# A hybrid decoder block on one core: mLSTM by chunks with a state, four GLA levels in blocks of 32, a rebuilt end, and sums of MLP weights made by adding transfers

## The chip, the core and the metric

The kernel runs on one NeuronCore of a Trainium2 chip. Five engines work at once on a shared on-chip memory of 128 partitions: TensorE (PE in the rows; its weight loads are PEld), VectorE (DVE), ScalarE (ACT), GpSimd (POOL) and SyncE (SP, which here only issues transfers). Each engine takes its own instructions strictly in order, and waits on semaphores for the others. PSUM is the memory that TensorE writes its products to. The metric is the device time of one execution in microseconds (us).

## What is computed

One layer (DEPTH = 1) of a decoder with 512 tokens of width 1024. Three token mixers work side by side on the normed input (mLSTM, GLA and gated DeltaNet, each with 4 heads of 128), are merged by sigmoid gates, and are followed by a squared-ReLU MLP of width 4096 and a last norm.

```
u = rmsnorm(x, g_norm_mix);  proj = u @ w_in            # q, k, v, gates of all three mixers
# mLSTM, per head, over chunks, with carried C, n, m
P   = exp(D - m_t) * (q k^T)                             # D from cumulated forget gates and input gates
num = P v + w_inter * (q C);  den = sum(P) + w_inter * (q n)
h   = num / max(|den|, exp(-m_t))
C   = w_old * C + (k * w_s)^T v                          # the state that the next chunk gets
# GLA, per head, decay per channel, b = cumsum(g) in a chunk
A[t,s] = sum_k q[t,k] exp(b[t,k] - b[s,k]) k[s,k]        # s <= t
o   = A v + (q exp(b)) S;   S = exp(bL) S + (k exp(bL - b))^T v
# gated DeltaNet: a triangular solve per chunk, then a state as above
x = x + (sum_n sigmoid(gate_n) * (branch_n @ w_up_n)) @ w_out
u = rmsnorm(x, g_norm_mlp)
x = x + square(relu(u @ w_mlp_in)) @ w_mlp_out
return rmsnorm(x, g_final)
```

## The kernel before

**Who sets the order.** The program is recorded as a graph of operations (`Graph.record`, L160), each with a cost per engine (`cost`, L207). `schedule` (L247) plays the graph through with these costs, and the order in which operations start there is the order in which each engine gets them (`emit`, L511). So nothing is ordered at run time: an instruction whose input is late holds up all that stands behind it on its engine. Large matmul groups ("mains") come in a fixed sequence of names (`plan`, L544 to L550); the small matmuls of the mixers are put between them when their inputs should be there. Buffers come in classes with a fixed count: the halves of a split weight (`wh`, `wl`) have 3 each, the mixers' PSUM banks (`m`) have 4.

**Products in fp32 by three.** Large products split each operand into a rounded half and a rest, and make three matmuls of 512 columns (`mm3`, L611). A weight that arrives by DMA is cast by ScalarE (`...h`) and its rest is made by VectorE (`...l`), as in `split_b`, L1438. Small products of the mixers are plain fp32 matmuls, which the trace shows as two instructions each.

**mLSTM** (`gen_mlstm`, L1133). No state is carried. For each head the 512 x 512 lower triangle of weighted scores is made in four block columns (`mqk`, with 512, 384, 256 and 128 columns), and ten products with the values (`mn`, 129 columns, the last of them for the denominator) follow.

**GLA** (`gen_gla`, L1205). Inside a chunk of 128 the lower triangle of A is made by levels of halves: at level L the queries of the second half and the keys of the first half of every stretch of 2L tokens are scaled to the border between them. Levels 64, 32 and 16 make small products, one for each stretch. Levels 8, 4, 2 and 1 make one product of 128 x 64 for each of four chunks (`ll`), of which a mask picks what counts (`copy_predicated` into `lAT`).

**MLP.** `mlp_in` (L1417) makes 512 hidden columns in four quarters (`mip`, 24 matmuls each). `mlp_out` (L1445) multiplies each such group with its part of the second weight by a scheme of Strassen and Winograd's kind, seven half-size products (`product`, 12 matmuls each, named P1 to P7; tiles `P` and `pp`) in place of eight. The four quarters of the weight, `b11` to `b22`, are transferred into the tile `em` by SP, and the four sums of quarters that the scheme needs are made by VectorE in place, as `em<-em`. Seven groups go this way, the eighth is `mlp_last` (L1529).

**End.** For each of four blocks of 128 tokens (t), two halves of 512 columns (hf): the last product is added to `x2`, ScalarE takes the squares' sum (`square_of`), and `finish` (L1563) makes the norm's factor `fy` from a square root on ScalarE and one Newton step on VectorE, multiplies by factor and weight (`gf`), and stores.

Of the kernel before, what the change touches and what calls it, by code (L numbers as in the profile page):

```python
# [113 lines left out]
class Graph:  # L114
# [92 lines left out]
    def cost(self, eng, method, a, k, op):  # L207
# [364 lines left out]
def write_block(nc, xT, w_cm, w_tm, w_sc, w_up, w_out, w_mi, w_mo, w_lr, prm, cst, g_fin, x_tm, out):  # L572
# [560 lines left out]
    def gen_mlstm(h):  # L1133
# [4 lines left out]
        pt = []  # L1138
        for j in range(4):
            e = nc.tile("w", [P, S], F32, f"me{h}{j}")  # L1140
            bias = a_c[:, h, j:j + 1]
            nc.scalar.activation(e[:, blk(j)], md[:, blk(j)], AF.Exp, bias=bias)
            if j < 3:
                nc.scalar.activation(e[:, (j + 1) * P:], nm[:, (j + 1) * P:], AF.Exp, bias=bias)
            pq = mps(f"mqk{h}{j}")
            mm(pq[:, j * P:], mk[h][:, blk(j)], mq[h][:, j * P:])
            nc.vector.tensor_mul(e[:, j * P:], e[:, j * P:], pq[:, j * P:])
            pt.append(e)
# [46 lines left out]
    hlT = []  # L1195
    cone = slot("cone")
# [8 lines left out]
    def gen_gla(h):  # L1205
        if h == 0:
            lrr = tmp("lrr")
            nc.sync.dma_start(lrr[:96], w_lr)
            nc.scalar.copy(lrw[:96], lrr[:96])
            nc.gpsimd.memset(cone, 1.0)  # L1210
            nc.gpsimd.memset(h4(cone)[:, :, 0:1], 0.0)
            nc.vector.tensor_sub(lrw[64:96], lrr[64:96], lrw[64:96].bitcast(F32))
# [32 lines left out]
        for li_, L in enumerate((64, 32, 16, 8, 4, 2, 1)):  # L1245
            nb = S // (2 * L)
            b3 = b.rearrange("p (n x) -> p n x", x=2 * L)
            w = nc.tile("w", [P, S], F32, f"lw{h}{L}")
            w3 = w.rearrange("p (n x) -> p n x", x=2 * L)
            k3 = lk[h].rearrange("p (n x) -> p n x", x=2 * L)  # L1250
            q3 = lq[h].rearrange("p (n x) -> p n x", x=2 * L)
            nc.vector.tensor_sub(w3[:, :, :L + 1], b3[:, :, L:L + 1].broadcast_to([P, nb, L + 1]), b3[:, :, :L + 1])
            if L > 1:
                nc.vector.tensor_sub(w3[:, :, L + 1:], b3[:, :, L + 1:], b3[:, :, L:L + 1].broadcast_to([P, nb, L - 1]))
            nc.scalar.activation(w, w, AF.Exp, scale=-1.0 / 16.0)
            q_ = q3[:, :, L:]
            if L > 1:
                wq = nc.tile("mq", [P, 256], F32, f"lwq{h}{L}").rearrange("p (n l) -> p n l", l=L)
                nc.vector.tensor_mul(wq, w3[:, :, L:], q_)
                q_ = wq  # L1260
            nc.vector.tensor_mul(w3[:, :, :L + 1], w3[:, :, :L + 1], k3[:, :, :L + 1])
            pl = mps(f"ll{h}{L}")
            p4 = pl[:, :256].rearrange("p (c n l) -> p c n l", c=4, l=L)
            nh = 64 // L
            if L >= 16:
                for c in range(4):
                    for i in range(nh):
                        o = c * P + i * 2 * L
                        mm(p4[i * 2 * L:i * 2 * L + L + 1, c, i], w[:, o:o + L + 1], q_[:, c * nh + i])
# [4 lines left out]
                for i in range(nh):  # L1274
                    r0 = i * 2 * L
                    nc.either.copy(A4[r0:r0 + L + 1, :, r0 + L:r0 + 2 * L], p4[r0:r0 + L + 1, :, i])
            else:
                for c in range(4):
                    mm(p4[:, c], w[:, blk(c)], q_[:, c * nh:(c + 1) * nh])
                nc.vector.copy_predicated(At.rearrange("p (c n x) -> p c n x", c=4, x=2 * L)[:, :, :, L:], lmask(li_ - 3), p4)  # L1280
# [92 lines left out]
    r2n = one("r2n", [P, 2])  # L1373
    r2c = one("r2c", [P, 4])

    def gen_x2():
# [14 lines left out]
        nc.vector.tensor_scalar_mul(r2n, r2c[:, 2:4], -1.0)  # L1391
# [53 lines left out]
    def mlp_out(g, a):  # L1445


        (a11, a21), (a12, a22) = a
        b11, b12, b21, b22 = bq
        for x, hf, i in ((b11, 0, 0), (b12, 1, 0), (b22, 1, 1), (b21, 0, 1)):  # L1450
            nc.sync.dma_start(x, w_mo[g, hf, i])

        tail = g == NG - 2
# [17 lines left out]
        product(1, a11, b11, "11")  # L1471
        if tail:
            for t in range(2):
                us[t] = slot(f"u{t}")
                nc.either.copy(us[t], p1[t])
        s1 = slot("S1")
        nc.vector.tensor_add(s1, a21, a22)
        nc.vector.tensor_sub(b11, b12, b11)
        for t, ps in enumerate(product(5, s1, b11, "S1")):
            if g == 0:  # L1480
                p5[t] = slot(f"P5{t}")
                nc.either.copy(p5[t], ps)
            else:
                nc.vector.tensor_add(p5[t], p5[t], ps)
        s2 = slot("S2")
        nc.vector.tensor_sub(s2, s1, a11)
        nc.vector.tensor_sub(a21, a11, a21)
        nc.vector.tensor_sub(b12, b22, b12)
        for t, ps in enumerate(product(7, a21, b12, "S3")):
            if g == 0:  # L1490
                p7[t] = slot(f"P7{t}")
                nc.either.copy(p7[t], ps)
            else:
                nc.vector.tensor_add(p7[t], p7[t], ps)
        nc.vector.tensor_sub(b11, b22, b11)
        product(6, s2, b11, "S2")
        if tail:
            join()
        s4 = slot("S4")
        nc.vector.tensor_sub(s4, a12, s2)  # L1500
        for t, ps in enumerate(product(3, s4, b22, "S4")):
            if tail:
                break
            nc.vector.scalar_tensor_tensor(x2[t][1], ps, r2c[:, t:t + 1], x2[t][1], op0=ALU.mult, op1=ALU.add)
        nc.vector.tensor_sub(b11, b11, b21)
        for t, ps in enumerate(product(4, a22, b11, "22")):
            nc.vector.scalar_tensor_tensor(x2[2 + t][0], ps, r2n[:, t:t + 1], x2[2 + t][0], op0=ALU.mult, op1=ALU.add)
        for t, ps in enumerate(product(2, a12, b21, "12")):
            if tail:
                break  # L1510
            nc.vector.scalar_tensor_tensor(x2[t][0], ps, r2c[:, t:t + 1], x2[t][0], op0=ALU.mult, op1=ALU.add)

    def join():

        def add(t, hf, v):
            nc.vector.scalar_tensor_tensor(x2[t][hf], v, r2c[:, t:t + 1], x2[t][hf], op0=ALU.mult, op1=ALU.add)

        for t in range(2):
            v = slot(f"v{t}")
            nc.vector.tensor_add(v, us[t], p6[t])  # L1520
            add(t, 0, us[t])
            nc.vector.tensor_add(us[t], v, p5[t])
            add(t, 1, us[t])
            nc.vector.tensor_add(p7[t], p7[t], v)
            add(2 + t, 0, p7[t])
            nc.vector.tensor_add(p5[t], p5[t], p7[t])
            add(2 + t, 1, p5[t])

    def mlp_last(a):  # L1529
# [10 lines left out]
        for hf, t, c0, n in [(hf, t, 0, 512) for t in range(3) for hf in range(2)] + [(0, 3, 0, 512), (1, 3, 0, 256), (1, 3, 256, 256)]:  # L1540
# [22 lines left out]
    def finish(t):  # L1563
# [31 lines left out]
    gf = [slot(f"gf{hf}") for hf in range(2)]  # L1595
    for hf in range(2):
# [82 lines left out]
```

## Time and profile before

| what | value |
|---|---|
| three runs | 953.68, 954.04 and 954.08 us, median 954.04 us |
| the profiled execution | 953.96 us |
| its span, first to last instruction | 952.1 us |
| TensorE busy | 942.1 us (99%) |
| VectorE, ScalarE, GpSimd busy | 647.3, 458.5 and 4.3 us |
| end of the last matmul | 943.2 us |

The profiled execution is 1.86 us longer than its span; that part lies outside the instructions. A chain of waits follows the program back from its last instruction, at each step to what released it; it is printed as pieces in order of time, each with its start, its length, the tile and the number of instructions, and it is the best clock for matmuls here, because their own durations overlap.

### The profile page before, as it was taken

The numbers are of one execution on the slowest core, as the hardware profiler recorded it, in microseconds if no ns is written. First come the engines' busy times: TensorE is split into PE (matmuls) and PEld (weight loads), VectorE is DVE, ScalarE is ACT, GpSimd is POOL, SyncE is SP. The second block draws the span as 40 slices with busy tenths as digits, with TensorE's granted clock in tenths as the row PEclk, the third lists the DMA queues.
The fourth block names the chain that finished last, engine by engine and source line by source line (L and its number), as shares of the span: only waits on it lengthen the run. The fifth ranks groups of instructions, "written<-read, shape, count | busy, mean of one in ns | idle before, by whom it ended". The sixth has DMA issues, their size and how long they took to land.

```text
span 952.1 us, 12788 instructions
## 1 busy us (share of the span) xinstructions
PE 942.1 (99%) x4890; PEld 786.2 (83%) x4890; DVE 647.3 (68%) x1146; ACT 458.5 (48%) x877; POOL 4.3 (0%) x18
## 2 busy tenths in 40 slices
PE   9999999999999999999999999999999999999996
PEld 8888888888888888888888888888888888888885
DVE  6766766777725755877735754556778687876886
ACT  6545465543533664455333334455446446545533
POOL 0000000000000000000000000000000000000000
PEclk9999999999999999999999999999999999999998
DMA  9222524122411422222233223213241335424002
GB/s 347 107 90 102 164 89 133 56 78 89 119 67 45 178 89 89 89 67 67 90 111 111 89 94 105 89 45 115 87 149 60 122 111 177 134 88 133 1 1 89
DMA packets 37941, 96.74 MB, mean 102 GB/s; under 512 B 7884, under 2 KB 12108, under 8 KB 37880
## 3 DMA queue, kind: packets, MB, share of 16 engines
q1 hardware_dynamic: 37592, 95.62, 30.4%
q8 instruction: 38, 0.62, 0.3%
q10 hardware_dynamic: 288, 0.30, 0.1%
q14 instruction: 23, 0.19, 0.1%
HBM read 93.27 MB, written 2.65 MB: 101 GB/s over the span
## 4 chain that ended last, share of the span: by engine, by line
PE 99%; DVE 0%; DVEq 0%; issue 0%
PE mip L533 18%; PE pp L533 9%; PE upp L533 7%; PE P L533 6%; PE wop L533 5%; PE mop L533 3%; PE mvp L533 3%; PE lrp L533 2%; PE dzp L533 2%; PE lvp L533 2%; PE ll L533 2%; PE gt21p L533 1%; PE gt13p L533 1%; PE gt20p L533 1%; PE gt22p L533 1%; PE gt12p L533 1%
## 5 line engine op out<-in xcount | busy, mean ns | idle before, releaser
L533 DVE TENSOR_TENSOR em<-em 128x1024 f32<-128x1024 f32 x28 | 34.1, 1219 | 0.1
L533 ACT ACTIVATE A<-rl 128x256 f32<-128x256 f32 x64 | 23.7, 411 | 3.2 <-DVE aS4l L533 2.0
L533 DVE SCALAR_TENSOR_TENSOR sg<-sg,upp 128x512 f32<-128x512 f32 x24 | 16.5, 686 | 11.9 <-PE upp L533 11.7
L533 DVE TENSOR_TENSOR lw<-lbs 128x260 f32<-128x260 f32 (+12 forms) x52 | 20.9, 448 | 4.9 <-PE ll L533 4.9
L533 ACT ACTIVATE rl<-mip 128x512 f32<-128x512 f32 x32 | 18.9, 590 | 6.3 <-PE mip L533 6.3
L533 DVE TENSOR_TENSOR P<-P,pp 128x512 f32<-128x512 f32 x24 | 16.2, 686 | 7.6 <-PE pp L533 7.4
L533 ACT ACTIVATE lw<-lw 128x512 f32<-128x512 f32 x28 | 17.6, 630 | 7.9 <-DVE lw L533 7.3
L533 PEld LDWEIGHTS ll<-lwq,lw 128*17 128x17 f32 (+3 forms) x320 | 17.5, 131 | 3.8 <-ACT lAT L533 1.8
L533 PE MATMUL ll<-lwq,lw 128*17 128x16 f32 (+3 forms) x320 | 18.2, 214 | 0.0
L533 DVE SCALAR_TENSOR_TENSOR x<-pp,r2c,x 128x512 f32<-128x512 f32 x24 | 16.9, 745 | 0.0
L533 DVE TENSOR_TENSOR x2T<-xr,wop 128x512 f32<-128x512 f32 x8 | 5.5, 687 | 16.3 <-PE wop L533 16.3
L533 ACT ACT_TABLE_LOAD x10 | 12.8, 1283 | 1.3 <-PEq L1667 1.2
L533 DVE TENSOR_TENSOR lw<-lw,lks 128x260 f32<-128x260 f32 (+6 forms) x28 | 13.1, 497 | 0.0
L533 DVE SCALAR_TENSOR_TENSOR x<-pp,r2n,x 128x512 f32<-128x512 f32 x14 | 10.5, 748 | 3.1 <-PE pp L533 3.1
L533 ACT COPY lAT<-ll 17x64 f32<-17x64 f32 (+3 forms) x32 | 7.1, 231 | 10.8 <-PE ll L533 10.4
L533 ACT ACTIVATE yh<-sg 128x512 fp32r<-128x512 f32 x8 | 5.0, 632 | 13.5 <-DVE sg L533 13.5
L533 DVE TENSOR_TENSOR me<-me,mqk 128x512 f32<-128x512 f32 (+3 forms) x16 | 7.7, 484 | 5.4 <-PE mqk L533 4.9
L533 ACT ACTIVATE fsq<-x 128x512 f32<-128x512 f32 (+1 forms) x9 | 5.3, 585 | 12.5 <-DVE x L533 12.5
L533 PEld LDWEIGHTS mn<-mv,me 128*128 128x128 f32 x80 | 10.0, 191 | 1.1 <-DVE smo L533 0.2
L533 DVE TENSOR_TENSOR sg<-sg,sg 128x512 f32<-128x512 f32 x16 | 10.8, 690 | 0.1
L533 PE MATMUL mqk<-mqs,mks 128*128 128x512 f32 (+3 forms) x32 | 10.7, 432 | 0.0
L533 ACT ACTIVATE cvs<-cv 128x512 f32<-128x512 f32 x12 | 7.5, 629 | 6.1 <-DVE cv L533 6.0
(1849 smaller groups left out, 3276.1 us busy)
## 6 DMA issues: line engine op xcount, KB each, us to landing
em<-in_w_mo_dram SPq DMA_DIRECT2D x28, 512.0 KB, 3.3
xk<-in_xT_dram SPq DMA_DIRECT2D x8, 256.0 KB, 5.3
em<-in_x_tm_dram SPq DMA_DIRECT2D x4, 512.0 KB, 8.4
em<-scr_rows SPq DMA_DIRECT2D x16, 128.0 KB, 5.0
xr<-in_xT_dram SPq DMA_DIRECT2D x8, 256.0 KB, 4.0
out_dram<-x SPq DMA_DIRECT2D x7, 256.0 KB, 2.4
nm<-scr_rows SPq DMA_DIRECT2D x4, 256.0 KB, 4.6
mo00r<-in_w_tm_dram SPq DMA_DIRECT2D x1, 512.0 KB
```

The lines of the kernel that those rows point to most:

```text
L533: getattr(getattr(nc, eng), method)(*[f(x) for x in a], **{n: f(x) for n, x in k.items()})
```

## The change

- **mLSTM.** The four block columns become four diagonal blocks of 128 x 128. What comes from earlier chunks goes through a state `C` for each head: the keys are transposed (`mkt`), scaled, multiplied with the values (`mu`), and the three results are chained on VectorE.
- **GLA.** Levels 8, 4, 2 and 1 make, instead of one product of 128 x 64 for each chunk, four products of 32 x 16, each for the diagonal block of 32 tokens that holds all its stretches. Levels are paired in one PSUM bank (32 with 16, 8 with 4, 2 with 1). The bank of a small pair is filled with zeros first by ScalarE. The products of a pair wait for the weights of both its levels (`nc.after`).
- **Costs and sequence.** The planner's table gets a line for such small products, and the MLP's products get another sequence.
- **MLP.** The scheme's signs are changed so that all sums of weights are sums. GpSimd issues transfers that add a quarter of the weight to what lies in `em` (`plus`), five for each group; VectorE's four `em<-em` go.
- **End.** For t < 3 GpSimd multiplies by `gf`, and ScalarE by the factor, where VectorE did both. The table for the square root is loaded earlier by a square root whose result is not used.

```
+            if n <= 16 and a[1].shape[-1] <= 33:
+                return 0.033, 0.2
...
-        seq += [... "c0 p1 p5 c1 p7 p6 c2 p3 p4 c3 p2" ...]
+        seq += [... ("c0 p1 p7 c1 p5 p6 c2 p4 p3 c3 p2" if g == 7 else "c0 p1 p7 c1 p3 p5 c2 p2 c3 p6 p4") ...]
...
-        for j in range(4):
-            e = nc.tile("w", [P, S], F32, f"me{h}{j}")
...
-            mm(pq[:, j * P:], mk[h][:, blk(j)], mq[h][:, j * P:])
-            nc.vector.tensor_mul(e[:, j * P:], e[:, j * P:], pq[:, j * P:])
+        for c in range(3):
+            tr(pk[:, blk(c)], mk[h][:, blk(c)])
+        nc.vector.tensor_mul(h4(kt)[:, :3], h4(pk)[:, :3], bc(x[:, 0:3]))
...
+        for c in range(4):
+            mm(pq[:, blk(c)], mk[h][:, blk(c)], mq[h][:, blk(c)])
+        nc.vector.tensor_mul(e, e, pq)
...
+        for c in range(3):
+            mm(pu[:, blk(c, P + 1)], kt[:, blk(c)], mv[c][:, h, :])
+        nc.either.copy(C[:, :P + 1], pu[:, :P + 1])
+        for c in (1, 2):
+            nc.vector.scalar_tensor_tensor(C[:, blk(c, P + 1)], C[:, blk(c - 1, P + 1)], x[:, 2 + c:3 + c], pu[:, blk(c, P + 1)], op0=ALU.mult, op1=ALU.add)
...
-                for j in range(t + 1):
-                    mm(n2[:, tt], pt[j][:, blk(t)], mv[j][:, h, :], start=(j == 0), stop=(j == t))
+                mm(n2[:, tt], e[:, blk(t)], mv[t][:, h, :], start=True, stop=(t == 0))
+                if t:
+                    mm(n2[:, tt], qe[:, blk(t)], C[:, blk(t - 1, P + 1)], start=False, stop=True)
...
+            if levels[0] < 16:
+                nc.scalar.copy(pl[:, :256 * len(levels)], zero[:, :256 * len(levels)])
...
-                for c in range(4):
-                    mm(p4[:, c], w[:, blk(c)], q_[:, c * nh:(c + 1) * nh])
+                        for i in range(4):
+                            n0 = c * nh + i * m
+                            prod(p4[blk(i, 32), c, i * m:(i + 1) * m], w[:, blk(4 * c + i, 32)], q_[:, n0:n0 + m])
...
+        def plus(q, hf, i):
+            nc.gpsimd.dma_start(q, w_mo[g, hf, i], accum_op=ALU.add)
+        load(x_, 0, 0)
+        load(y_, 1, 0)
+        plus(y_, 1, 1)
...
-        nc.vector.tensor_sub(b11, b12, b11)
-        nc.vector.tensor_sub(b12, b22, b12)
-        nc.vector.tensor_sub(b11, b22, b11)
-        nc.vector.tensor_sub(b11, b11, b21)
+        def p_1():
+            product(1, a11, x_, "11")
+            plus(x_, 1, 0)
...
+        def p_5():
+            keep_sum(p5, 5, product(5, s1, x_, "S1"))
+            plus(x_, 1, 1)
+        def p_7():
+            keep_sum(p7, 7, product(7, a21, y_, "S3"))
+            plus(y_, 0, 0)
+            plus(y_, 0, 1)
...
+            if t < 3:
+                nc.gpsimd.tensor_mul(o, o, gf[hf])
...
-                nc.vector.scalar_tensor_tensor(x2[t][hf], x2[t][hf], y, gf[hf], op0=ALU.mult, op1=ALU.mult)
+                    nc.scalar.mul(x2[t][hf], x2[t][hf], y)
...
+    nc.follow(prev[1][1])
+    nc.scalar.activation(root, r2c[:, 0:1], AF.Sqrt)
```

What this does to the order of instructions is shown at three places. First TensorE between the gates' products of the second branch, where the small GLA levels of the first head stand. `ll` is the levels' PSUM bank, `lwq` and `lw` are the scaled queries and keys, `gt22p` and `gt13p` are gate products of 512 columns. Before:

```order
L533 MATMUL gt22p_3690<-xl,gt220h 128x512
L533 MATMUL gt22p_3690<-xh,gt220h 128x512
L533 MATMUL ll_3768<-lwq_3290,lw_3250 128x64 x4
L533 MATMUL gt22p_3690<-xh,gt220l 128x512
L533 MATMUL gt22p_3690<-xl,gt220h 128x512
```

And now:

```order
L535 MATMUL gt13p_3865<-xl,gt130h 128x512
L535 MATMUL gt13p_3865<-xh,gt130h 128x512
L535 MATMUL ll_3850<-lwq_3413,lw_3359 32x16 x16
L535 MATMUL gt13p_3865<-xh,gt130l 128x512
L535 MATMUL gt13p_3865<-xl,gt130h 128x512
```

One level is now 16 products of 32 x 16 in one run where it was 4 of 128 x 64. Of the sixteen such levels, twelve stand alone between large products, three stand next to products of another level that are cut small too, and one is cut in two by transposes; before, ten runs held the sixteen levels.

Second VectorE in the MLP, around the split of the sum that P7 multiplies with (`b2S3` before, `b3S3` now; `em` is the tile with the weights, `aS..` and `S` are halves and sums on the other side, `mi31` and `mi41` the next quarter of the first MLP weight). Before:

```order
L533 TENSOR_TENSOR b2S1l<-em,b2S1h 128x1024
L533 TENSOR_TENSOR aS1l<-S_6422,aS1h 128x512
L533 TENSOR_TENSOR mi31l<-mi31r,mi31h 128x1024
L533 TENSOR_TENSOR A_6143<-A_6138,A_6143 128x512
L533 TENSOR_TENSOR em<-em 128x1024
L533 TENSOR_TENSOR P_5847<-P_5847,pp_6464 128x512
L533 TENSOR_TENSOR P_5868<-P_5868,pp_6479 128x512
L533 TENSOR_TENSOR b2S3l<-em,b2S3h 128x1024
```

And now:

```order
L535 TENSOR_TENSOR b311l<-em,b311h 128x1024
L535 TENSOR_TENSOR b3S3l<-em,b3S3h 128x1024
L535 TENSOR_TENSOR aS3l<-A_6718,aS3h 128x512
L535 TENSOR_TENSOR S_6993<-S_6934,A_6728 128x512
L535 TENSOR_TENSOR aS1l<-S_6934,aS1h 128x512
L535 TENSOR_TENSOR S_7005<-A_6872,S_6993 128x512
L535 TENSOR_TENSOR a12l<-A_6872,a12h 128x512
L535 TENSOR_TENSOR aS2l<-S_6993,aS2h 128x512
L535 TENSOR_TENSOR mi41l<-mi41r,mi41h 128x1024
```

The sum `em<-em` is gone from VectorE. The split `b3S3l` now comes from what an adding transfer left, at the beginning of the group, and six halves and sums and the split of `mi41` stand behind it.

Third VectorE at the very end of the program (`x_5631` before and `x_5858` now are the right half of the last block of tokens, `fs`, `fv`, `fy` the steps to the norm's factor). Before:

```order
L533 RECIPROCAL fy<-fs 128x1
L533 SCALAR_TENSOR_TENSOR x_5426<-x_5426,fy,gf_7230 128x512
L533 TENSOR_SCALAR fs<-fy,fv,fs 128x1
L533 SCALAR_TENSOR_TENSOR x_5602<-x_5602,fy,gf_7249 128x512
L533 RECIPROCAL fy<-fs 128x1
L533 SCALAR_TENSOR_TENSOR x_5433<-x_5433,fy,gf_7230 128x512
L533 SCALAR_TENSOR_TENSOR x_5609<-x_5609,fy,gf_7249 128x512
L533 SCALAR_TENSOR_TENSOR x_5631<-x_5631,fy,gf_7249 128x256
L533 TENSOR_SCALAR x_5631<-x_5631,fy 128x256
```

And now:

```order
L535 TENSOR_TENSOR fv<-fss,fe 128x1
L535 RECIPROCAL fy<-fs 128x1
L535 TENSOR_SCALAR fs<-fy,fv,fs 128x1
L535 RECIPROCAL fy<-fs 128x1
L535 SCALAR_TENSOR_TENSOR x_5858<-x_5858,fy,gf_7727 128x256
L535 TENSOR_SCALAR x_5858<-x_5858,fy 128x256
```

Four products of 512 columns that belong to earlier blocks have left VectorE from between the steps of the last block.

## Rows read from the trace of the kernel before

**Rows 1.** The page: busy time of each engine, and the ending chain by engine.

```profile
PE 942.1 (99%) x4890; PEld 786.2 (83%) x4890; DVE 647.3 (68%) x1146; ACT 458.5 (48%) x877; POOL 4.3 (0%) x18
...
PE 99%; DVE 0%; DVEq 0%; issue 0%
```

**Rows 2.** Busy time by stretch: the MLP, and what follows the last matmul.

```profile
core 0: us, PE busy (x) PEld busy (x) DVE busy (x) ACT busy (x) POOL busy (x), PEclk, DMA share, GB/s
...
640.00:925.00 285.00, 285.00 (x1259) 236.04 (x1259) 215.66 (x260) 143.95 (x221) 0.00 (x0) 1.00 0.30 98
...
943.20:952.10 8.90, 0.00 (x0) 0.00 (x0) 5.22 (x14) 1.53 (x4) 0.00 (x0) 0.61 0.54 206
```

**Rows 3.** The chain, in the mLSTM: start us, length us, tile, instructions.

```profile
150.80 1.94 PE mqk L533 x6
...
161.17 2.23 PE mn L533 x20
...
164.10 0.44 PE pk L533 x4
...
176.78 0.22 PE mqk L533 x2
```

**Rows 4.** The chain in GLA, first head: level 16, then level 8.

```profile
394.88 0.32 PE ll L533 x32
395.19 1.59 PE gt22p L533 x6
396.78 0.84 PE ll L533 x8
397.62 6.89 PE gt22p L533 x30
```

**Rows 5.** The chain in gated DeltaNet: products of 32 x 32.

```profile
260.16 1.13 PE pY L533 x64
```

**Rows 6.** The chain in the MLP: a quarter of the hidden columns, and a half-size product.

```profile
687.37 5.44 PE mip L533 x24
692.81 2.72 PE pp L533 x12
```

**Rows 7.** DMA issues: engine, operation, count, KB each, us to landing.

```profile
em<-in_w_mo_dram SPq DMA_DIRECT2D x28, 512.0 KB, 3.3
...
em<-in_x_tm_dram SPq DMA_DIRECT2D x4, 512.0 KB, 8.4
```

**Rows 8.** Groups of VectorE, 640 to 920 us: busy us, mean ns of one.

```profile
L533 DVE TENSOR_TENSOR em<-em 128x1024 f32<-128x1024 f32 x25 | 30.5, 1218 | 0.0
...
L533 DVE TENSOR_TENSOR aS3l<-A,aS3h 128x512 fp32r<-128x512 f32 x7 | 4.8, 687 | 0.0
...
L533 DVE TENSOR_TENSOR mi12l<-mi12r,mi12h 128x1024 fp32r<-128x1024 f32 x1 | 1.2, 1226 | 1.9 <-ACT mi12h L533 1.9
```

**Rows 9.** Groups of ScalarE there: the cast that makes a weight's rounded half.

```profile
L533 ACT CAST mi60h<-mi60r 128x1024 fp32r<-128x1024 f32 x1 | 1.1, 1057 | 1.7 <-PE pp L533 1.7
```

**Rows 10.** VectorE at the end, in order of time: start us, length us.

```profile
944.76 0.16 DVE L533 RECIPROCAL fy<-fs 128x1 f32<-128x1 f32 x1
944.84 0.73 DVE L533 SCALAR_TENSOR_TENSOR x<-x,fy,gf 128x512 f32<-128x512 f32 x1
945.49 0.27 DVE L533 TENSOR_SCALAR fs<-fy,fv,fs 128x1 f32<-128x1 f32 x1
945.67 0.74 DVE L533 SCALAR_TENSOR_TENSOR x<-x,fy,gf 128x512 f32<-128x512 f32 x1
946.33 0.16 DVE L533 RECIPROCAL fy<-fs 128x1 f32<-128x1 f32 x1
946.40 1.79 DVE L533 SCALAR_TENSOR_TENSOR x<-x,fy,gf 128x512 f32<-128x512 f32 x3
948.11 0.35 DVE L533 TENSOR_SCALAR x<-x,fy 128x256 f32<-128x256 f32 x1
```

**Rows 11.** Groups of GpSimd, over the whole span: the longest.

```profile
L533 POOL MEMSET lAT<- 128x512 f32 x4 | 2.0, 527 | 82.0 <-DVE dz L533 81.5 <-PE upp L533 0.5
```

More of the change, by code (lines that the diff above doesn't have):

```diff
@@ L1210, in gen_gla @@
             nc.gpsimd.memset(cone, 1.0)
+            nc.gpsimd.memset(zero, 0.0)
             nc.gpsimd.memset(h4(cone)[:, :, 0:1], 0.0)
@@ new lines, in gen_gla, with prod @@
+        for levels in ((64,), (32, 16), (8, 4), (2, 1)):
+            lw, lq_ = {}, {}
+            for L in levels:
+                nb = S // (2 * L)
+                b3 = b.rearrange("p (n x) -> p n x", x=2 * L)
+                w = nc.tile("w", [P, S], F32, f"lw{h}{L}")
+                w3 = w.rearrange("p (n x) -> p n x", x=2 * L)
+                k3 = lk[h].rearrange("p (n x) -> p n x", x=2 * L)
+                q3 = lq[h].rearrange("p (n x) -> p n x", x=2 * L)
+                nc.vector.tensor_sub(w3[:, :, :L + 1], b3[:, :, L:L + 1].broadcast_to([P, nb, L + 1]), b3[:, :, :L + 1])
+                if L > 1:
+                    nc.vector.tensor_sub(w3[:, :, L + 1:], b3[:, :, L + 1:], b3[:, :, L:L + 1].broadcast_to([P, nb, L - 1]))
+                nc.scalar.activation(w, w, AF.Exp, scale=-1.0 / 16.0)
+                q_ = q3[:, :, L:]
+                if L > 1:
+                    wq = nc.tile("mq", [P, 256], F32, f"lwq{h}{L}").rearrange("p (n l) -> p n l", l=L)
+                    nc.vector.tensor_mul(wq, w3[:, :, L:], q_)
+                    q_ = wq
+                nc.vector.tensor_mul(w3[:, :, :L + 1], w3[:, :, :L + 1], k3[:, :, :L + 1])
+                lw[L], lq_[L] = w, q_
+            pl = mps(f"ll{h}{levels[0]}")
+            if levels[0] < 16:
+                nc.scalar.copy(pl[:, :256 * len(levels)], zero[:, :256 * len(levels)])
+            def prod(o, a, q_):
+                nc.after(lw[levels[-1]])
+                mm(o, a, q_)
+            for n, L in enumerate(levels):
+                w, q_ = lw[L], lq_[L]
+                p4 = pl[:, blk(n, 256)].rearrange("p (c n l) -> p c n l", c=4, l=L)
+                nh, m = 64 // L, 16 // L
+                for c in range(4):
+                    if L >= 16:
+                        for i in range(nh):
+                            o = c * P + i * 2 * L
+                            prod(p4[i * 2 * L:i * 2 * L + L + 1, c, i], w[:, o:o + L + 1], q_[:, c * nh + i])
+                    else:
+                        for i in range(4):
+                            n0 = c * nh + i * m
+                            prod(p4[blk(i, 32), c, i * m:(i + 1) * m], w[:, blk(4 * c + i, 32)], q_[:, n0:n0 + m])
@@ L1372, in write_block @@
     ss2 = one("ss2", [P, 8])
-    r2n = one("r2n", [P, 2])
+    r2n = one("r2n", [P, 4])
     r2c = one("r2c", [P, 4])
@@ L1448, in mlp_out, with load @@
         (a11, a21), (a12, a22) = a
-        b11, b12, b21, b22 = bq
-        for x, hf, i in ((b11, 0, 0), (b12, 1, 0), (b22, 1, 1), (b21, 0, 1)):
-            nc.sync.dma_start(x, w_mo[g, hf, i])
+        x_, y_, b21, b22 = bq
+        def load(q, hf, i):
+            nc.sync.dma_start(q, w_mo[g, hf, i])
+        def plus(q, hf, i):
[3 more added lines that the diff above has]
+        plus(y_, 1, 1)
+        load(b22, 1, 1)
+        load(b21, 0, 1)
         tail = g == NG - 2
@@ L1469, in product @@
             return out_
[L1471 to L1477, printed above, removed]
-        nc.vector.tensor_sub(b11, b12, b11)
[L1479 to L1484, printed above, removed]
@@ L1508, in mlp_out, with keep_sum @@
[L1508 to L1511, printed above, removed]
+        def p_1():
+            product(1, a11, x_, "11")
+            plus(x_, 1, 0)
+            if tail:
+                for t in range(2):
+                    us[t] = slot(f"u{t}")
+                    nc.either.copy(us[t], p1[t])
+        def keep_sum(acc, n, out_):
+            for t, ps in enumerate(out_):
+                if g == 0:
+                    acc[t] = slot(f"P{n}{t}")
+                    nc.either.copy(acc[t], ps)
+                else:
+                    nc.vector.tensor_add(acc[t], acc[t], ps)
@@ new lines, in p_5, with p_6, p_3 @@
+        def p_5():
[5 more added lines that the diff above has]
+            plus(y_, 0, 1)
+        def p_6():
+            product(6, s2, x_, "S2")
+            if tail:
+                join()
+        def p_3():
+            for t, ps in enumerate(product(3, s4, b22, "S4")):
+                if not tail:
+                    nc.vector.scalar_tensor_tensor(x2[t][1], ps, r2c[:, t:t + 1], x2[t][1], op0=ALU.mult, op1=ALU.add)
@@ new lines, in p_4, with p_2 @@
+        def p_4():
+            for t, ps in enumerate(product(4, a22, y_, "22")):
+                nc.vector.scalar_tensor_tensor(x2[2 + t][0], ps, r2c[:, 2 + t:3 + t], x2[2 + t][0], op0=ALU.mult, op1=ALU.add)
+        def p_2():
+            for t, ps in enumerate(product(2, a12, b21, "12")):
+                if not tail:
+                    nc.vector.scalar_tensor_tensor(x2[t][0], ps, r2c[:, t:t + 1], x2[t][0], op0=ALU.mult, op1=ALU.add)
+        s1, s2, s4 = slot("S1"), slot("S2"), slot("S4")
@@ L1518, in join @@
         for t in range(2):
             v = slot(f"v{t}")
[L1520 to L1525, printed above, removed]
+            nc.vector.tensor_sub(v, p6[t], us[t])
+            add(t, 0, us[t], r2c)
+            nc.vector.tensor_sub(us[t], v, p5[t])
+            add(t, 1, us[t], r2c)
+            nc.vector.tensor_sub(p7[t], p7[t], v)
@@ L1526, in join @@
+            add(2 + t, 0, p7[t], r2c)
             nc.vector.tensor_add(p5[t], p5[t], p7[t])
-            add(2 + t, 1, p5[t])
+            add(2 + t, 1, p5[t], r2n)
     def mlp_last(a):
@@ L1595, in write_block @@
     gf = [slot(f"gf{hf}") for hf in range(2)]
+    root = small("root", 1)
+    nc.follow(prev[1][1])
+    nc.scalar.activation(root, r2c[:, 0:1], AF.Sqrt)
     for hf in range(2):
```

91 lines of the change are left out of this document (33 added, 58 removed).

## The prediction

> **What bounds the kernel now.** I read the page first: TensorE is busy 942.1 of 952.1 us, and the ending chain lies on it for 99% [rows 1]. The windows show the same stage by stage. In the MLP TensorE has 285.00 busy of 285.00 us, at a granted clock of 1.00 (the upper level, 2.4 GHz), while VectorE has 215.66 and ScalarE 143.95; after the last matmul 8.90 us are left in which TensorE does nothing [rows 2]. So only three things move the time: matmul work that goes, the end behind the last matmul, and a wait that appears on TensorE. Work taken from VectorE is worth nothing by itself. The profiled execution (953.96) lies 0.08 below the median of the three runs (954.04), so what is taken off the one is taken off the other; 1.86 of it lie outside the span and stay. As small matmuls overlap, I price them by the chain's lengths, not by single durations.
>
> **mLSTM: −3.8.** Before, one head has 512+384+256+128 columns of scores: 1.94 + 0.22, and ten products with the values, 2.23 [rows 3]; together 4.39. After, it has three transposes (four take 0.44, so 0.33), four blocks of 128 x 128 (0.22 each for two instructions, so 0.88), three products for the state and seven with values and state, 129 columns each, as two instructions of 2.23/20 = 0.1115: 3 x 0.223 = 0.67 and 7 x 0.223 = 1.56 [rows 3]. That is 3.44, or 0.95 less; for four heads 3.8. The state adds a serial way through VectorE (keys scaled, product, copy, two chained sums) before the values' products. TensorE waits there only if no large product is due; groups of 512 columns stand between the steps, so I take 0 for it.
>
> **GLA: −6.1.** A level of four 128 x 64 products costs 0.84 in the chain, and the large products after it take 6.89 for 30 where 30 at the MLP's 0.2267 (5.44/24) make 6.80, so 0.09 more for the restart: 0.93 [rows 4, 6]. A level that is already cut small, 16 products of 17 x 16, is in the same chain: 0.32, and the six large ones behind it take 1.59 where six make 1.36: 0.23 for the restart [rows 4]. So a level alone goes from 0.93 to 0.55. By sessions: ten runs held the sixteen levels before, some 16 x 0.84 + 10 x 0.09 = 14.3. After, twelve stand alone (12 x 0.55 = 6.6), three beside other small products (3 x 0.32 = 1.0) and one is cut by transposes (about 0.6): 8.2. The difference is 6.1. Rows of the new size itself (32 x 16) are not there. The row on the other side is gated DeltaNet's 32 x 32: 64 instructions in 1.13, so 32 in 0.565, with the restart 0.79 a level [rows 5]; 0.14 saved for each of sixteen, 2.2. I take 6.1, because the moved columns (16) are those of the 0.32 row and only the weights are wider; the bound 2.2 stays as a rival. ScalarE's filling of banks with zeros and the masks on VectorE cost nothing on the chain as long as they are done before the bank's second level, and large matmuls stand between the two levels of a bank.
>
> Against such blocks there is a rule in the Trainium skill ("TensorEngine Tiling (Array Packing)", Instruction Overhead): a matmul has some 60 cycles of overhead whatever its width, so tiling shouldn't take from a dimension that is already small. By it 32 instructions of 16 columns would cost 32 x 60 cycles at 2.4 GHz, 0.80 (an estimate by that page), more than the trace shows for the same count. The trace doesn't agree: 32 instructions in 0.32, 10 ns each [rows 4].
>
> **MLP: 0.** The products stay seven of 2.72 for each group; VectorE loses four sums of 1218 ns for each (30.5 in all for 25) [rows 6, 8], off the chain. Instead, five transfers for each group add to what lies in `em`. The trace has none, so the latency L of one is the unknown. Nearest rows: a plain 512 KB load of the same weight lands in 3.3, the slowest 512 KB row in 8.4 [rows 7]. An adding one reads two sources and writes one, three moves where a load has two: 3.3 x 1.5 = 5.0, which I take as an estimate, nearer the first row since tile and weight are the same; 8.4 is the upper bound.
>
> How long may it take? Count from the start of P7 (sequence c3 p6 p4 | c0 p1 p7). The tile for the next group's first sum is free after the split of the quarter that P4 uses. Three buffers let that begin when P2 ends, 19.04 ahead of P7 (5.44 + 2.72 + 2.72 + 5.44 + 2.72 [rows 6]). Add the split (cast 1.06 [rows 9], rest 1.23 [rows 8], with hand-overs about 3), the plain load 3.3, and 0.3 between: the adding transfer can begin at −12.4. What must be ready after it is not P7 alone: VectorE takes its queue in order, and behind `b3S3l` stand six halves and sums of 0.69 and the split of `mi41` (1.23), which c1 needs at +2.72. So the sum must have landed at 2.72 − 6 x 0.69 − 2 x 1.23 − 1.06 − 0.2, about −5.1. That leaves L up to 7.3 free. In the last group P6 follows P5 directly on a twice-added `x_`: from the end of P5's split, at about the start of c1, to P6 there are 5.44 + 2.72, less 2.6 for P6's split, so L up to 5.6 is free. The stall in all is 6 x (L − 7.3) + (L − 5.6), each where positive. At 5.0 it is 0; at 6.6 (two plain loads) 1.0; at 8.4 it is 6.6 + 2.8 = 9.4. GpSimd's queue takes the adds in order: the first stands ahead of the memsets of `lAT`, 0.53 each [rows 11], but its tile is loaded long before the GLA levels at 394.88 [rows 4], so I take 0.
>
> On what an adding transfer costs the Trainium skill has a rule ("Collectives: The Full Stack", The bandwidth ceiling): an add has two source reads on one ring, and moves at about half the rate of a copy (ratio 1.93). By it L would be at most about 6.4, and the time 0.8 later than my sum; no run shown here has an adding transfer.
>
> **End: −2.1.** VectorE's way from the first RECIP of `fy` at 944.76 to the end of the last scaling at 948.46 is 3.70. Its own steps are RECIP 0.16, TS 0.27, RECIP 0.16, half-width STT (three STTs in 1.79, two of them 0.66 each, so about 0.47) and TS 0.35: 1.41. Between them stand four STTs of 512 columns for earlier blocks [rows 10], which leave. So 2.3 less; I take 2.1, as ScalarE now has two scalings of block 2 ahead of the last squares and waits for GpSimd's products. GpSimd's price for a 512-column product is unknown: from the same on VectorE (0.69 [rows 8]) to three times its own 512-column memset (3 x 0.53 = 1.6 [rows 11]). Up to about 2.4 it is done before the last matmul; I take 1.6 and no wait.
>
> **Sum.** 3.8 + 6.1 + 2.1 = 12.0; 954.04 − 12.0 = **942.0**.
>
> **Rivals.**
> - *The adding transfer shows a little* (L 7.5 to 8.8): TensorE waits at each group's turn; at 8.4 the sum becomes 942.0 + 9.4 = 951.4. For it: the 8.4 row [rows 7]. Against: that row is of another load, at the start.
> - *Slower than before: the adding transfer is late.* Its price is the stall above; break-even with the 12.0 is at L = 8.8, that is 2.7 plain loads, and at 10.5 it is 6 x 3.2 + 4.9 = 24, so 966. For it: seven group turns, no slack on TensorE (285.00 of 285.00 [rows 2]), and the price not in the trace. Against: DMA is busy 0.30 of the MLP [rows 2].
> - *The 32-row blocks cost what 32 x 32 costs* [rows 5]: GLA gives 2.2 in place of 6.1, so 945.9. If a level's time didn't fall with the cut at all (still 0.84, and 0.23 of restart [rows 4]), it would cost 1.07, 0.14 more than before: 16 x 0.14 = 2.2 lost and 6.1 not won, 950.3; 10 ns a product speaks against it, so I give that 0.02. It is what the tiling page of the Trainium skill, named above, would lead to.
> - *The end gives nothing*: GpSimd needs over 2.4 a product, or VectorE and GpSimd hold each other up: 944.1.
> - *The mLSTM's part doesn't come*, since its serial way through VectorE (busy there too) holds TensorE for as long as it saves: 945.8, the edge of the forecast's own range.
>
> **How the numbers follow.** Forecast 0.67 (940 to 945.8: bounds of restart, L up to 7.5). Transfer shows a little 0.12, of which 0.09 below 952.1 and 0.03 at no change. Late transfer 0.10, of which 0.02 near no change. 32-row blocks dear 0.07 (0.05 for 945.9, 0.02 for 950.3). End 0.04. A measurement of this kernel can tell about 0.2% (1.9 us) from no change. Faster: 0.67 + 0.09 + 0.07 + 0.04 = 0.87; same 0.05; slower 0.08. For 8 in 10 the range leaves out the late transfer and the top of the small one, and goes from 940.0 to 950.0.
>
> **What would show it.** GLA: in the chain `ll` pieces of about 0.3 where 0.84 stood, and restarts of 0.2. mLSTM: `mqk`, `mn`, `mu` and transposes near 3.4 a head. MLP: TensorE again without idle time, and the issues of `em` on GpSimd's queue near 5.0; wrong if TensorE waits for a cast `..S3h` or `..S2h` that waits for a transfer. End: from the last matmul to the span's end 6.8 in place of 8.9, GpSimd's products under 2.4. The forecast falls if these transfers take over 7.3, or if the chain shows a new wait in the mixers.

## The result, and the profile after

The changed kernel takes 943.3 us in the median of four runs (943.06 to 943.64); the kernel before took 953.92 beside it (953.68 to 954.08). The ratio is 0.9889, with an interval of 0.9872 to 0.9906: 10.6 us faster. The forecast was 942.0, with a range of 940.0 to 950.0. The profiled execution of after took 943.64, its span is 941.9; the span of before was 952.1, so 10.2 us are to be found in the two traces.

The page of after, in the parts that answer to [rows 1] and [rows 7] (busy time by engine; the ending chain by engine; DMA issues with count, KB and us to landing):

```profile
PE 933.4 (99%) x5286; PEld 775.3 (82%) x5286; DVE 617.9 (66%) x1127; ACT 470.5 (50%) x905; POOL 43.6 (5%) x60
...
PE 97%; DVE 1%; DMA 1%; issue 1%; ACT 0%; POOL 0%; DVEq 0%; ACTq 0%; POOLq 0%
...
em<-in_w_mo_dram POOLq DMA_DIRECT2D x35, 512.0 KB, 6.6
em<-in_w_mo_dram SPq DMA_DIRECT2D x28, 512.0 KB, 3.8
```

TensorE is busy 8.7 us less and still sets the time, but its share of the chain is 97% where it was 99%, and a DMA is there. An adding transfer takes 6.6 in the median where a plain load takes 3.8.

The chain in the mLSTM of after (start us, length us, tile, instructions), to be held against [rows 3]:

```profile
137.85 0.66 PE mkt L535 x6
...
139.90 0.89 PE mqk L535 x8
...
141.49 0.67 PE mu L535 x6
...
150.95 0.89 PE mn L535 x8
```

Six transposes (three for each of two heads) take 0.66, a head's four score blocks 0.89, its three state products 0.67, and eight instructions with the values 0.89; every instruction takes a little over 0.11. Large products stand between these four pieces.

The chain in GLA of after, against [rows 4]:

```profile
393.33 0.32 PE ll L535 x32
393.65 5.68 PE gt22p L535 x24
...
400.01 0.38 PE ll L535 x32
400.39 6.34 PE gt13p L535 x27
```

The first pair is level 16, as before. The second is a level cut into blocks of 32 x 16: 0.38 where 0.84 stood, and the 27 large products behind it take 6.34 where 27 x 0.2267 make 6.12, so 0.22 for the restart.

What TensorE waited for in after (us in all, times, longest), and the chain at that place:

```profile
PE P L535 <- DVE b6S2l L535: 0.8, 1, 0.8
```

```profile
880.98 0.02 POOLq L535
881.00 0.86 POOL em L535
881.86 0.10 issue
881.96 7.02 DMA em<-in_w_mo_dram
...
889.05 1.06 ACT b6S2h L535
...
890.13 1.24 DVE b6S2l L535
...
891.41 2.81 PE P L535 x11
```

Here, in the last MLP group, P6 waits: GpSimd issues an adding transfer, another right behind it, which takes 7.02, then ScalarE casts, VectorE makes the rest, and P6 goes on at 891.41. From one matmul's end to the next it is 0.46 and then 1.25 where 0.227 is usual, so 1.26 are lost.

The end, by stretch (columns as in [rows 2]), and VectorE's last steps and GpSimd's products, against [rows 10]:

```profile
935.20:941.90 6.70, 0.00 (x0) 0.00 (x0) 2.45 (x9) 1.52 (x4) 0.00 (x0) 0.64 0.20 80
```

```profile
936.60 0.16 DVE L535 RECIPROCAL fy<-fs 128x1 f32<-128x1 f32 x1 [0.17 <-ACT fs L535]
936.80 0.27 DVE L535 TENSOR_SCALAR fs<-fy,fv,fs 128x1 f32<-128x1 f32 x1
937.11 0.16 DVE L535 RECIPROCAL fy<-fs 128x1 f32<-128x1 f32 x1
937.30 0.48 DVE L535 SCALAR_TENSOR_TENSOR x<-x,fy,gf 128x256 f32<-128x256 f32 x1
937.71 0.34 DVE L535 TENSOR_SCALAR x<-x,fy 128x256 f32<-128x256 f32 x1
```

```profile
L535 POOL TENSOR_TENSOR x<-x,gf 128x512 f32<-128x512 f32 x6 | 8.4, 1406 | 41.2 <-ACT fsq L535 41.2
```

From the first RECIP to the last scaling it is 1.45 (936.60 to 938.05) where it was 3.70. The tail is 6.70 where it was 8.90.

**The account.** For the mixers I add up, over every run of small matmuls, the time from the end of the large matmul ahead of it to the end of the large one behind it, less 0.227: 98.5 us before, 89.6 after, 8.9 less. With the tail (8.95 to 6.69 from the last matmul's modelled end, 2.26 less) and the new wait (1.26 more) that is 9.9 of the 10.2.

### The profile page after: what moved, and what is told of

It reads as the page before. It is cut to its first block, busy times and chain, and to the rows that moved or that the text cites. A ratio compares the mean times of both kernels' runs of the same rounds, so it can differ in the third digit from the quotient of the medians.

```text
span 941.9 us, 13685 instructions
## 1 busy us (share of the span) xinstructions
PE 933.4 (99%) x5286; PEld 775.3 (82%) x5286; DVE 617.9 (66%) x1127; ACT 470.5 (50%) x905; POOL 43.6 (5%) x60
## 4 chain that ended last, share of the span: by engine, by line
PE 97%; DVE 1%; DMA 1%; issue 1%; ACT 0%; POOL 0%; DVEq 0%; ACTq 0%; POOLq 0%
PE mip L535 17%; PE pp L535 9%; PE upp L535 7%; PE P L535 5%; PE wop L535 5%; PE mop L535 3%; PE mvp L535 3%; PE lrp L535 3%; PE lvp L535 2%; PE dzp L535 2%; PE ll L535 1%; PE gt12p L535 1%; PE gt21p L535 1%; PE gt22p L535 1%; PE gt13p L535 1%; PE lk0p L535 1%
## 5 line engine op out<-in xcount | busy, mean ns | idle before, releaser
L535 POOL DMA_DIRECT2D em<-in_w_mo_dram x35 | 30.4, 869 | 482.4 <-DVE b011l L535 238.7
L535 DVE SCALAR_TENSOR_TENSOR x<-pp,r2c,x 128x512 f32<-128x512 f32 x38 | 27.1, 744 | 2.4 <-PE pp L535 2.4
L535 PEld LDWEIGHTS ll<-lwq,lw 128*32 128x32 f32 (+3 forms) x608 | 9.4, 109 | 6.9 <-issue 5.3
L535 DVE COPY_PREDICATED lAT<-cs,ll 128x256 f32<-128x256 uint8 x16 | 9.3, 582 | 5.3 <-PE ll L535 5.3
L535 ACT COPY lAT<-ll 17x64 f32<-17x64 f32 (+3 forms) x32 | 7.0, 231 | 10.6 <-PE ll L535 10.3
L535 PE MATMUL ll<-lwq,lw 128*32 128x16 f32 (+3 forms) x608 | 11.5, 187 | 0.0
L535 ACT CAST aS2h<-S 128x512 fp32r<-128x512 f32 x7 | 4.3, 621 | 12.6 <-DVE S L535 12.6
L535 POOL TENSOR_TENSOR x<-x,gf 128x512 f32<-128x512 f32 x6 | 8.4, 1406 | 41.2 <-ACT fsq L535 41.2
L535 DVE TENSOR_TENSOR lwq<-lw,lqs 128x256 f32<-128x256 f32 x24 | 9.8, 423 | 0.3
L535 DVE TENSOR_TENSOR Z<-Z,tmU 64x30 f32<-64x30 f32 (+14 forms) x30 | 9.6, 318 | 0.2
```

What stands on the lines that cost most here:

```text
L535: getattr(getattr(nc, eng), method)(*[f(x) for x in a], **{n: f(x) for n, x in k.items()})
```

## The experiments

**Each part alone.** Four kernels, each the kernel before with one part of the diff.

The mLSTM part:

```diff
-        for j in range(4):
-            mm(pq[:, j * P:], mk[h][:, blk(j)], mq[h][:, j * P:])
+        for c in range(4):
+            mm(pq[:, blk(c)], mk[h][:, blk(c)], mq[h][:, blk(c)])
```

> The kernel before with the mLSTM part alone. My sum: 3.8 us less, 950.1 (0.9960). The trace of after, from matmul to matmul, gives the mLSTM's small products 17.56 before and 13.79 after, 3.77 less. Rival: the serial way through VectorE takes part of it back when the other parts are not there, 951 to 954.

950.01 (949.94 to 950.51), ratio 0.9960 (0.9948 to 0.9973): 3.9 less. The sum over runs of small matmuls falls from 98.5 to 94.7, 3.8. The serial way through VectorE costs nothing that can be seen.

The GLA part:

```diff
-                    mm(p4[:, c], w[:, blk(c)], q_[:, c * nh:(c + 1) * nh])
+                            prod(p4[blk(i, 32), c, i * m:(i + 1) * m], w[:, blk(4 * c + i, 32)], q_[:, n0:n0 + m])
```

> The kernel before with the GLA blocks and the planner's cost line alone. The prediction's term: 6.1 us less, 947.8. From the trace of after, where a level alone costs 0.576 in place of 0.895: 16 x 0.895 = 14.3 against some 9.1, 5.2 less, 948.7 (0.9945). Rival by the 32 x 32 rows: 2.2 less, 951.7.

948.04 (947.84 to 948.38), ratio 0.9940 (0.9927 to 0.9952): 5.9 less, near the prediction's 6.1. The sum over small matmuls is 92.6, 5.9 less. So the two parts alone take 3.8 and 5.9 off that sum, 9.7, and together 8.9. The missing 0.8 belongs to neither: added to the mLSTM part, GLA gives 5.1; added to the GLA part, the mLSTM gives 3.0. It goes with the number of runs: 102 before and with the mLSTM alone, 103 with GLA alone, 108 with both, and a run pays a restart of some 0.2. That the planner's order makes more runs is seen; that their count is the whole cause, and why it splits them so, was not tried.

The MLP part (adding transfers, signs, sequence):

```diff
-        nc.vector.tensor_sub(b12, b22, b12)
+            nc.gpsimd.dma_start(q, w_mo[g, hf, i], accum_op=ALU.add)
```

> The kernel before with the MLP part alone (adding transfers, signs, sequence). My account: no gain, and the wait of the last group, L - 5.6 with L = 6.6, so 1.0 to 1.3 more: 955.1 (1.0012). Rival: the MLP part gains by itself, under 953.7, or costs nothing, 953.9.

953.51 (953.02 to 954.27), ratio 0.9997 (0.9988 to 1.0006): no difference that these runs can tell, though the trace has two. The only new wait, and the stretches around it and after the last matmul:

```profile
PE P L533 <- DVE aS4l L533: 1.0, 1, 1.0
```

```profile
909.11 1.10 issue
910.21 0.75 DVE x L533
910.96 0.61 DVE aS4l L533
911.57 0.14 issue
911.71 2.97 PE P L533 x12
```

```profile
944.70:951.70 7.00, 0.05 (x1) 0.00 (x0) 3.17 (x11) 1.80 (x6) 0.00 (x0) 0.81 0.38 150
```

A wait of 1.0 (1.28 lost from matmul to matmul) is there, as expected, but from another cause: a half of a sum, `aS4l`, stands behind other work in VectorE's queue, and no transfer is in it. And the tail is 7.0 in place of 8.9 although the end's code is that of before. With the new sequence VectorE ends the last group's sums (`P<-P,P`) 14.5 us ahead of the last matmul where it was 11.1, and the four scalings that stood between the last block's steps in [rows 10] are all done ahead of its first RECIP. The tail is 1.96 shorter, and the wait gives 1.28 of it back.

The end alone:

```diff
+            if t < 3:
+                nc.gpsimd.tensor_mul(o, o, gf[hf])
...
-                nc.vector.scalar_tensor_tensor(x2[t][hf], x2[t][hf], y, gf[hf], op0=ALU.mult, op1=ALU.mult)
+                    nc.scalar.mul(x2[t][hf], x2[t][hf], y)
```

> The kernel before with the end alone (GpSimd's products, ScalarE's scalings, the table's early load). My term: 2.1 less, 951.8 (0.9978); after's trace has 2.26 less from the last matmul to the span's end. Rival: the gain needs the other parts, 953 to 954.

952.1 (951.85 to 952.6), ratio 0.9981 (0.9972 to 0.9990): 1.8 less. The tail:

```profile
943.40:950.50 7.10, 0.00 (x0) 0.00 (x0) 2.44 (x9) 2.30 (x6) 0.00 (x0) 0.65 0.47 185
```

The four parts alone make 3.9 + 5.9 + 0.4 + 1.8 = 12.0, the whole change 10.6. The MLP's sequence and the rebuilt end shorten the same tail: by 1.96 and 1.83 alone, by 2.26 together.

**Each of these two taken out of the changed kernel.** The edits are the same hunks, the MLP's and the end's, put back to what the kernel before has.

> The changed kernel with the MLP of before (VectorE's sums, old signs, old sequence). If the last group's wait (1.25 us from matmul to matmul, where 0.23 is usual) belongs to the adding transfers and the end alone brings VectorE free, as in the run of the end alone (7.12 from last matmul to the span's end, 6.69 now): 943.3 - 1.05 + 0.43 = 942.7. Rival, the parts add up: without the MLP's 0.4 it is 943.7.

Without the MLP part: 943.3 (four times, two at 942.8 and two at 943.8), the same as with it. The median decides for neither of the two numbers expected. The profiled execution (942.8) has no wait in the MLP, and 7.05 behind the last matmul, so in the two traces the MLP part costs 1.26 at P6 and takes 0.36 off the tail. The adding transfers bring nothing to the time: with the sums of 1218 ns back on VectorE [rows 8] TensorE waits for none of them.

> The changed kernel without the rebuilt end. If the MLP part's sequence and the end buy the same 2 us at the tail (the MLP alone has 6.99 from last matmul to the span's end, the end alone 7.12, before 8.94, both 6.69): 943.3 + 0.3 = 943.6. Rival, the parts add up: 943.3 + 1.8 = 945.1.

Without the end: 944.87 (944.31 to 946.36), 1.6 more. That is near the rival's number, but not for its reason. The tail is 6.9, so the end gives the tail 0.2 only. What TensorE waits for in the MLP now is this:

```profile
PE P L535 <- DVE aS4l L535: 0.9, 1, 0.9
PE P L535 <- DVE b6S2l L535: 0.8, 1, 0.8
```

The wait for `aS4l` is back, 1.12 from matmul to matmul. The planner had put `aS4l` ahead of the split of `mi73` on VectorE when the end was rebuilt (899.5 and 900.8), and puts it behind without that (902.6 and 901.0): a change at the end moved the order 20 us earlier.

**What P6 waits for.** Nothing but the order of two of GpSimd's transfers is changed, in the last group:

```diff
         def p_7():
             plus(y_, 0, 0)
-            plus(y_, 0, 1)
+            if not tail:
+                plus(y_, 0, 1)
         def p_5():
             plus(x_, 1, 1)
+            if tail:
+                nc.gate = [nc.ops[-1]]
+                plus(y_, 0, 1)
```

> The changed kernel; in the last MLP group alone GpSimd issues the second add into x_ (which P6 waits for) ahead of the second add into y_ (which P4 needs later). Same instructions, no other order changed. If the transfer is what P6 waits for: 0.9 us earlier issue and part of the shared DMA time, the wait of 1.0 goes to 0 to 0.3, 942.3 to 942.6. Rival, VectorE's or ScalarE's queue holds P6: 943.3.

942.75 (942.34 to 943.13), ratio to before 0.9883 (0.9869 to 0.9898). The transfer that P6 needs is issued at the same 882.0, and not 0.9 earlier as expected: its tile is free only when the split for P5 ends, at 881.7 in both. But it takes 5.5 where it took 7.0 behind the other one. The DMA rows of the two issues, of after and of this kernel (count, KB, us to landing):

```profile
em<-in_w_mo_dram POOLq DMA_DIRECT2D x1, 512.0 KB, 7.0
```

```profile
em<-in_w_mo_dram POOLq DMA_DIRECT2D x1, 512.0 KB, 5.5
```

And the chain of this kernel has no wait between P5 (`pp`) and P6 (`P`):

```profile
887.48 2.72 PE pp L535 x12
890.20 2.72 PE P L535 x12
```

The wait came from the transfer being the second of two under way at once. Its time differs by execution: in four other kernels that keep the two in the order of after (the one without the end, and three below: with one band, and twice with the products back on VectorE) it takes 6.3 to 6.5, and 0.6 to 1.0 are lost at P6. The span falls by 1.3, the median by 0.55, less than a measurement of this kernel can tell for sure; it is the fastest of all kernels run here.

**How late may the first sum be?** The transfer that adds for P7 is issued twice, one behind the other; then again, with a quarter of the tile the second time. The order on all engines is that of after.

```diff
         plus(y_, 1, 1)
+        nc.ops[-1].calls.append(nc.ops[-1].calls[0])          # whole tile
...
+        nc.ops[-1].calls.append(("gpsimd", "dma_start", (y_[:, 0, :256], w_mo[g, 1, 1, :, 0, :256]), dict(accum_op=ALU.add)))          # quarter
```

> The changed kernel with the first adding transfer of each MLP group (into y_, the sum for P7) issued twice, one behind the other; no order changed. The sum then holds that quarter twice, so the MLP's output is another one. The prediction's window formula: the transfer is free up to L = 7.3, then 6 x (L - 7.3) are lost. Twice some 5.5 makes L about 11: 6 x 3.7 = 22, so 965. Rival, there is far more room than I counted: 943 to 948.

> As the last one, but only a quarter of the tile (256 of 1024 columns) is added a second time; the MLP's output is another one here too. L some 5.5 and 2.5 to 3.5 for the small one, 8 to 9: 6 x 0.7 to 6 x 1.7, 947.5 to 953.5. Rival, more room: 943.3. With the run before, the two times give the slope and where it begins.

974.17 and 955.02, one execution each. The chain at the first group's turn, the stretch around its P7, in the run with the whole tile:

```profile
660.08 1.24 DVE b022l L535
661.32 0.02 issue
661.34 3.58 DMA em<-in_w_mo_dram
...
665.20 0.86 POOL em L535
...
670.81 5.58 DMA em<-in_w_mo_dram
...
676.46 1.06 ACT b1S3h L535
677.52 0.02 issue
677.54 1.23 DVE b1S3l L535
678.77 0.60 DVE aS3l L535
...
682.30 1.23 DVE mi21l L535
683.53 0.04 issue
683.57 2.56 PE mip L535 x10
```

This is the way that the prediction drew: split of the quarter for P4, plain load, adding transfer, cast and rest, VectorE's queue with its halves, the split of the next weight, and only then the matmuls that wait. Here L is 11.18 (665.20 to 676.38) and 3.1 are lost at this turn (1.75 at P7, 1.34 at the next quarter, each from matmul to matmul less 0.227). With the quarter tile L is 8.67 and 0.56 are lost. Both put the point from which it counts at 8.1, with a slope of 1; the prediction had 7.3. At the next three turns L less the loss is 7.8 to 8.0 in both runs; at the last two it is higher, 9.0 to 9.4 where anything is lost, and why was not tried.

974 is 9 more than the 965 expected. The later turns lose up to 4.6, as transfers beside each other slow down and L grows to 13.2. P6 of the last group loses 4.9 (4.3 with the quarter tile): its transfer stands in GpSimd's queue behind the second one into `y_`, which now comes late, and is issued 2.5 after the split for P5 in place of 0.3. Also 2.7 of the 31 us are lost in the first 27 us of the span, which the edit doesn't touch. And in the run with the whole tile some 3 us are the clock, 2 of them here:

```profile
914.50:918.00 3.50, 0.52 (x3) 0.09 (x1) 0.00 (x0) 0.79 (x1) 0.00 (x0) 0.97 0.55 108
918.00:924.00 6.00, 5.22 (x11) 3.76 (x12) 5.38 (x6) 3.15 (x5) 0.00 (x0) 0.50 0.00 0
924.00:930.00 6.00, 6.00 (x26) 4.92 (x25) 4.89 (x7) 1.67 (x2) 0.00 (x0) 0.95 0.00 0
```

After a wait of 3.9 us the granted clock is 0.50 (the lower level, 1.2 GHz) for some 6 us, and a 512-column matmul takes 0.427 in place of 0.227. In after's wait of 1.26 it stays at 1.00.

**What makes 32 x 16 cheap.** The four blocks of a chunk write to the same 32 partitions of PSUM (other columns), in place of four different bands of 32.

```diff
-                            prod(p4[blk(i, 32), c, i * m:(i + 1) * m], w[:, blk(4 * c + i, 32)], q_[:, n0:n0 + m])
+                            prod(p4[blk(0, 32), c, i * m:(i + 1) * m], w[:, blk(4 * c + i, 32)], q_[:, n0:n0 + m])
```

> The changed kernel with the four blocks of 32 tokens of a chunk writing to the same 32 PSUM partitions (different columns) in place of four different bands of 32. Leaves the small levels' results in wrong rows. If a small product's price comes from its size (32 x 16) alone: 943.3. If TensorE gets through the four bands side by side, 32 instructions take up to four times the 0.52 that they take now above the restart: 16 levels x up to 1.0 to 1.6 more, 960 to 970.

954.76 in one execution, 11.5 more, with the order of instructions unchanged. The sum over small matmuls goes from 89.6 to 101.4. The chain:

```profile
399.96 1.12 PE ll L535 x32
401.08 6.34 PE gt13p L535 x27
```

The same 32 instructions take 1.12 in place of 0.38: 35 ns each, not 12. With a restart of 0.2, a level costs 1.3, more than the 0.9 of the product of 128 x 64 that it replaces, and the GLA part would lose 6 us. So it is not the size alone that makes the small products cheap: neighbours in four different bands overlap. That each band has a lower bound for one instruction is the simplest reading, but it isn't shown; only 32-row bands were tried.

**GpSimd's products given back to VectorE**, at the same places of the order.

```diff
+                if (eng, method) == ("gpsimd", "tensor_mul"):
+                    eng = "vector"
```

> The changed kernel, GpSimd's six products at the end given to VectorE at the same places of the order; nothing else moves. VectorE gets 6 x 0.69 = 4.1 us more between 924 and 936, where it was idle for some 5 us. If the end's gain is that these products aren't on VectorE: the tail grows by 0.7 (the last one stands between the last block's steps), up to 2, 944 to 945. If only the order and ScalarE's scalings matter: 943.3.

> The last kernel again (GpSimd's six products done by VectorE at the same places of the order), since its four times lay at 943.5 and at 947.0 and its profile had the tail unchanged at 6.69. If GpSimd's products buy nothing: 943.3 to 943.6 in all runs. If they buy the tail: 944 to 945. If the spread of 3.5 us comes with the kernel and not with that chip, it is seen again.

The first time 945.15, with two of four at 943.5 and two at 947.0, which decides nothing; the second time 943.68 (943.3 to 944.6). The profiled executions (943.44 and 943.84) both have 6.69 from the last matmul to the span's end, as after has. So GpSimd's products buy nothing by themselves: VectorE had the room for them. The 3.5 us of the first four stay open. The end has two more hunks, ScalarE's scalings and the early load of the square root's table, and neither was run alone. The load is a rival for a share of the gain, since in the kernel before it stands between the squares and the square roots of earlier blocks, 6.7 ahead of the last matmul's end:

```profile
936.46 1.28 ACT L533 ACT_TABLE_LOAD   x1
```

With the end alone it starts 20.1 ahead. With the MLP part alone it starts 12.2 ahead though the end's code is that of before, and the tail is short there too. So which of the scalings, the load and the order shortens the end is not shown.

## Why the prediction was right, and where it was off

- **mLSTM, −3.8.** Measured alone 3.9, in the trace 3.8. The price by instruction of [rows 3] was all that was needed, and the serial way through VectorE made no wait on TensorE.
- **GLA, −6.1.** Alone 5.9; with the mLSTM part 0.8 of the two together is missing. Two terms of the sum were mis-sized. One is the level itself, 0.38 + 0.22 in the chain for the 0.32 + 0.23 taken, 0.05 a level, though the part alone lacks only 0.2 of its 6.1. The other was put at nothing: that the two parts change the planner's order for each other. The six more runs with small levels (sixteen where ten were) the prediction had counted. The rivals of 2.2 and of a loss fell: 32 x 16 costs nearly what 17 x 16 costs (0.38 and 0.32), not the 0.565 of [rows 5].
- **The rule that was set aside.** The prediction weighed a rule of the Trainium skill ("TensorEngine Tiling (Array Packing)", Instruction Overhead: some 60 cycles a matmul, so don't cut a dimension that is already small) against 10 ns an instruction and gave it a chance of 0.02. That was right for this kernel, but the reading too short: with all blocks in one band the trace has 35 ns an instruction, 1.12 for 32 where the prediction's estimate by the Trainium skill's figure was 0.80, and the cut loses, as that rule has it. With four bands the trace has 12 ns, less than that rule allows.
- **End, −2.1.** The tail is 2.26 shorter, near the sum, but that is partly luck. The reason given, four scalings gone from VectorE, is true of the rows, but the sum credited the end with all of it. The new MLP sequence alone, which the sum put at nothing, shortens the tail by 2.0, the end alone by 1.8. In the changed kernel the end takes 0.2 more off the tail, and some 1.1 elsewhere by the order of `aS4l`. GpSimd's product took 1.4 (1.6 taken, free up to 2.4).
- **MLP, 0.** Here lies a miss of 1.3, the larger part of the 1.8 by which the traces (10.2) fall short of the 12.0. The step that failed is the size of L, taken as one number. An adding transfer alone takes 5.3 to 5.6 in after (5.0 taken; 5.0 to 5.3 in the run of the MLP part alone), but 7.0 when it is the second of two. The formula for the last group, L − 5.6, was the right one: by 7.0 it gives 1.4 and the trace has 1.26; with 5.5, in the run with the two exchanged, it gives 0 and the trace has 0; in the four kernels with 6.3 to 6.5 it gives 0.7 to 0.9 and the traces have 0.6 to 1.0. The point of 7.3 for the other turns is about 8 or more by two runs; L stayed under it at those turns.
- **The ratio for an add.** "Collectives: The Full Stack" of the Trainium skill (The bandwidth ceiling) gives an add 1.93 times the moving time of a copy, measured on the two halves of a ring collective. For a single transfer, here, it is 5.5 against 3.4 to 3.6, 1.6 for the whole time to landing; the median of all (6.6 against the 3.3 of before) is 2.0, but that holds transfers that overlap. The adding ones are issued by GpSimd and the plain ones by SyncE, and no plain load by GpSimd was run, so how much of the 1.6 is the adding isn't shown.
- **"Work taken from VectorE is worth nothing by itself."** True of the sums `em<-em`: the MLP part taken out changes nothing (943.3 with and without). Not true where a queue feeds TensorE closely: `aS4l` alone cost 1.1 to 1.3 in two kernels because of what stood ahead of it.
- **The slower side.** The late transfer was the rival with 0.10. The runs show that its mechanism is real: some 3 and 6 us more at one transfer of each group made 955 and 974, in good part by what that set off at P6. The kernel lies some 2.5 us on the good side of that point at the turns (7.8 to 8.1, against an L of 5.4 to 5.6 for that transfer in after).

## What to carry to other kernels

Before a masked product is cut into diagonal blocks, see that the blocks land in different bands of 32 rows, where they overlapped here; count the restarts of the large products around them, not only the small products. Parts that shorten the same tail don't add up, so take each one alone before crediting it. When transfers replace an engine's work, what decides is the one transfer that the next product waits for: issue it ahead of those with time to spare.

## What the runs showed that was not expected

- Two adding transfers under way at once slow each other: about 5.5 alone, 6.3 to 7.0 as the second in the last group, up to 9.4 with four plain loads beside them (at 800 us of after), of which the one into `em` takes 6.2 there and about 3.5 alone.
- A planner that works by costs hands a change on: the rebuilt end, at 924 to 942, decided where `aS4l` stood at 900, and so a wait of 1.1. Parts that are priced one by one change each other's order.
- After a wait of 1.26 TensorE's granted clock stays at 1.00; after one of 3.9 it was 0.50 for about 6 us.
